# Row softmax on one core: which block of a tile's rows a partition takes

## The chip, the cores and the metric

The kernel runs on one core of a Trainium2 chip. The time is that of the device, in microseconds. A run is told by its median over repeated executions; the profile is of one execution. The core has 128 partitions of on-chip memory, VectorE (DVE in the profile), ScalarE (ACT), GpSimd (POOL) and SyncE (SP), and sixteen DMA engines that move data between the chip's memory and the partitions. TensorE is not used.

## The reference

The input is 32 x 512 rows of 1024 float32 numbers, so 16384 rows and 67.11 MB; the output has the same shape. Each row is divided by the temperature 0.5 and put through a softmax:

```python
scaled = x / temperature
shifted = scaled - np.max(scaled, axis=-1, keepdims=True)
exp_x = np.exp(shifted)
return (exp_x / np.sum(exp_x, axis=-1, keepdims=True)).astype(np.float32)
```

A row needs nothing of another row, so it doesn't matter which partition works on it, if the result goes back to its place.

## The kernel before

The 16384 rows are cut into eleven tiles, one after the other in memory: ten of 1536 rows and a last one of 1024 (`PASSES`, L10). A tile has 128 partitions with 12 rows (the last: 8) in each, 48 KB (32 KB) a partition. Four buffers hold tiles (`BUFS`, L11); a result overwrites its input in the buffer.

`dram(t, i)` (L50) gives the part of the input or the output that belongs to tile i, as partitions x rows x columns. Partition p takes the p-th block of 12 rows, so that the 128 blocks lie in memory in the order of the partitions and the tile is one contiguous stretch of 6144 KB (4096 KB). Both the load (L60) and the store (L108) use it, with one DMA for each tile.

Compute goes in groups of 4 or 6 rows per partition. `maximum` (L63) reduces each row on VectorE (L69) and scales the result into a bias (L72); `exponential` (L74) runs one ScalarE instruction per row (L78), with the row's sum as a by-product; `divide` (L87) takes reciprocals (L90) and multiplies on VectorE, in one instruction for a group (L93) in some tiles and row by row (L96) in the others.

The order is written out by hand (L113 to L127). Four loads are issued at the start. Then each group's maximum and exponential are followed by the division of the group before; in the last two tiles, for their first groups, that division comes ahead. When a tile's last group is divided, `store` issues its store, from GpSimd's queue for the first six tiles and from ScalarE's queue for the last five, and then `load()` issues the load of the next tile on SyncE's queue, which waits until the store that frees the buffer has landed. Ahead of the first store, a one-column copy on GpSimd (L106) holds that queue until the third tile has arrived.

Of the kernel before, what the change touches and what calls it, by code (L numbers as in the profile page):

```python
# [1 line left out]

# [4 lines left out]

PASSES = [[4, 4, 4]] + [[6, 6]] * 9 + [[4, 4]]  # L10
BUFS = 4  # L11

WHOLE = (2, 3, 4, 6, 8)


BY_POOL = 6

ALONE = 9


@with_exitstack
def kernel(
    ctx: ExitStack,
    tc: tile.TileContext,
    x: bass.AP,
    temperature: bass.AP,
    out: bass.AP,
):
    nc = tc.nc
    f32 = mybir.dt.float32  # L30
    scale = 1.0 / float(temperature)
    extreme = mybir.AluOpType.max if scale > 0 else mybir.AluOpType.min

    P = 128
    xf = x.flatten_outer_dims()
    of = out.flatten_outer_dims()
    n, d = xf.shape
    rows = [sum(ks) for ks in PASSES]
    assert sum(rows) * P == n

    data = ctx.enter_context(tc.tile_pool(name="data", bufs=BUFS))
    stats = ctx.enter_context(tc.tile_pool(name="stats", bufs=4))


    groups = []
    for i, ks in enumerate(PASSES):
        for j, k in enumerate(ks):
            groups.append((i, sum(ks[:j]), k))

    def dram(t, i):  # L50
        block = t[P * sum(rows[:i]) : P * sum(rows[: i + 1]), :]
        return block.rearrange("(p k) d -> p k d", p=P, k=rows[i])

    tiles, small = [], []

    def load():
        i = len(tiles)
        if i < len(PASSES):
            xt = data.tile([P, rows[i], d], f32, name="xt")
            nc.sync.dma_start(out=xt, in_=dram(xf, i))  # L60
            tiles.append(xt)

    def maximum(g):  # L63
        i, a, k = groups[g]
        top, bias, sums, recip = (
            stats.tile([P, k], f32, name=name) for name in ("top", "bias", "sums", "recip")
        )
        small.append((bias, sums, recip))
        nc.vector.tensor_reduce(  # L69
            out=top, in_=tiles[i][:, a : a + k, :], axis=mybir.AxisListType.X, op=extreme  # L70
        )
        nc.vector.tensor_scalar_mul(bias, in0=top, scalar1=-scale)  # L72

    def exponential(g):  # L74
        i, a, k = groups[g]
        bias, sums, _ = small[g]
        for b in range(k):
            nc.scalar.activation(  # L78
                tiles[i][:, a + b, :],
                tiles[i][:, a + b, :],  # L80
                mybir.ActivationFunctionType.Exp,
                bias=bias[:, b : b + 1],
                scale=scale,
                accum_out=sums[:, b : b + 1],
            )

    def divide(g):  # L87
        i, a, k = groups[g]
        _, sums, recip = small[g]
        nc.vector.reciprocal(recip, sums)  # L90
        if i in WHOLE:
            xt = tiles[i][:, a : a + k, :]
            nc.vector.tensor_mul(xt, xt, recip.unsqueeze(2).to_broadcast([P, k, d]))  # L93
            return
        for b in range(k):
            nc.vector.tensor_scalar_mul(  # L96
                tiles[i][:, a + b, :], in0=tiles[i][:, a + b, :], scalar1=recip[:, b : b + 1]
            )

    def store(g):  # L100
        i, a, k = groups[g]
        if a + k == rows[i]:
            if i == 0:


                nc.gpsimd.tensor_copy(stats.tile([P, 1], f32, name="seen"), tiles[2][:, 0, 0:1])  # L106
            queue = nc.gpsimd if i < BY_POOL else nc.scalar
            queue.dma_start(out=dram(of, i), in_=tiles[i])  # L108
            load()

    with tc.manual_schedule():  # L113
        for _ in range(BUFS):
            load()
        for g in range(len(groups) + 1):

            alone = g < len(groups) and groups[g][0] >= ALONE and groups[g][1] == 0
            if g > 0 and alone:
                divide(g - 1)  # L120
                store(g - 1)
            if g < len(groups):
                maximum(g)
                exponential(g)
            if g > 0 and not alone:
                divide(g - 1)
                store(g - 1)  # L127


# [1 line left out]
_INS = ['x', 'temperature']  # L131
_OUTS = [((32, 512, 1024), 'float32')]

_NUMBERS = {'temperature': 0.5}


# [26 lines left out]
```

## Time and profile before

| what | value |
|---|---|
| median of 3 runs | 317.14 us (317.06 to 317.22) |
| span of the profiled execution | 315.8 us |
| bytes read and written | 67.11 MB and 67.11 MB |
| mean rate over the span | 425 GB/s |
| load of 6144 KB, issue to landing | 36.4 us (median of 10) |
| store of 6144 KB, issue to landing | 35.9 us (GpSimd's queue), 31.9 us (ScalarE's) |
| last store (4096 KB), issue to landing | 13.5 us |

The span runs from the first to the last instruction of one profiled execution; the runs' median is 1.3 us longer. In the profile a queue is named by a number: q1 carries SyncE's loads, q0 GpSimd's stores, q10 ScalarE's stores. A packet is a piece that one DMA engine moves at a time. The row marked DMA gives, for 40 equal slices of the span, the mean busy share of the sixteen DMA engines in tenths. In the table by stretches, the columns after the interval are its length, the busy time and number of instructions of VectorE, ScalarE and GpSimd, the granted clock, the DMA engines' busy share and the rate in GB/s; a packet is counted where it starts, so that a short stretch's rate and share (1.05, say) are rough by a packet on each engine.

### The profile page before, as it was taken

To read this page: it belongs to the slowest core of one execution; us is meant where nothing else is said; L and a number is where in the kernel's file an instruction comes from. 1 tells how busy PE (TensorE), PEld (TensorE's weight loads), DVE (VectorE), ACT (ScalarE), POOL (GpSimd) and SP (SyncE) were. 2 spreads that over 40 slices of the span, in tenths; PEclk is the share of its full clock that TensorE was granted. 3 is DMA by queue.
4 is the path that set the end of the run, shared out by engine and by line. 5 is a ranking of instruction groups with operands and counts; after the bars stand their busy time and mean duration, and the time that the engine had idled before them with its cause. 6 is when DMAs were issued, how large, how long until landed. Compare 5 with 4: busy or idle time off the path is not lost.

```text
span 315.8 us, 525 instructions
## 1 busy us (share of the span) xinstructions
DVE 256.9 (81%) x147; ACT 148.3 (47%) x257; POOL 3.7 (1%) x11
## 2 busy tenths in 40 slices
DVE  0069999999999899979976994999199999969710
ACT  0029636775461807344471744074416802953700
POOL 0000001000000000000000000000000000000000
DMA  8999999999999999999999999999999999999996
GB/s 305 473 417 423 461 411 399 399 468 430 400 479 417 417 461 411 430 467 405 442 448 399 455 442 405 467 424 417 461 417 430 455 401 463 411 452 411 455 411 270
DMA packets 3171, 134.24 MB, mean 425 GB/s; under 512 B 352, under 2 KB 352, under 8 KB 352
## 3 DMA queue, kind: packets, MB, share of 16 engines
q1 hardware_dynamic: 1584, 67.11, 49.7%
q0 software_dynamic: 864, 37.75, 27.6%
q10 hardware_dynamic: 720, 29.36, 21.5%
q14 instruction: 3, 0.02, 0.0%
HBM read 67.11 MB, written 67.11 MB: 425 GB/s over the span
## 4 chain that ended last, share of the span: by engine, by line
DMA 47%; DVE 28%; ACT 11%; issue 9%; DVEq 0%; SPq 0%; POOLq 0%
DMA xt<-in_x_dram 25%; DMA out_dram<-xt 22%; DVE top L69 16%; ACT xt L78 11%; DVE xt L96 8%; DVE xt L93 2%; DVE bias L72 0%; DVE recip L90 0%; DVEq L158 0%; SPq L60 0%; POOLq L108 0%
## 5 line engine op out<-in xcount | busy, mean ns | idle before, releaser
L78 ACT ACTIVATE xt<-xt,bias 128x1024 f32<-128x1024 f32 x128 | 145.2, 1135 | 131.7 <-DVE recip L90 70.6
L69 DVE TENSOR_REDUCE top<-xt 128x6 f32<-128x6144 f32 (+1 forms) x23 | 139.9, 6083 | 37.8 <-DMA xt<-in_x_dram 37.8
L93 DVE TENSOR_TENSOR xt<-xt,recip 128x6144 f32<-128x6144 f32 x10 | 65.6, 6558 | 0.4
L96 DVE TENSOR_SCALAR xt<-xt,recip 128x1024 f32<-128x1024 f32 x68 | 46.2, 749 | 0.5
L78 ACT ACTIVATION_READ_ACCUMULATOR xt<-xt,bias 128x1 f32 x128 | 23.9, 187 | 0.0
L78 ACT ACT_TABLE_LOAD x1 | 1.3, 1283 | 18.3 <-DMA xt<-in_x_dram 18.3
L90 DVE RECIPROCAL recip<-sums 128x6 f32<-128x6 f32 (+1 forms) x23 | 4.2, 182 | 5.0 <-ACT xt L78 5.0
L108 POOL DMA_DIRECT2D out_dram<-xt x6 | 3.3, 554 | 129.6 <-ACT xt L78 82.7
L72 DVE TENSOR_SCALAR bias<-top 128x6 f32<-128x6 f32 (+1 forms) x23 | 3.9, 171 | 0.8
L106 POOL COPY seen<-xt 128x1 f32<-128x1 f32 x1 | 0.2, 185 | 46.9 <-DMA xt<-in_x_dram 46.9
L144 POOL MEMSET const-uint8-127<- 128x1 uint8 x1 | 0.1, 103 | 0.0
L144 POOL MEMSET const-bfloat16-1.0<- 128x1 bf16 x1 | 0.1, 102 | 0.0
L144 POOL MEMSET const-float32-0.0<- 128x1 f32 x1 | 0.1, 99 | 0.2 <-issue 0.2
L144 POOL MEMSET const-float32-1.0<- 128x1 f32 x1 | 0.1, 98 | 0.0
## 6 DMA issues: line engine op xcount, KB each, us to landing
xt<-in_x_dram SPq DMA_DIRECT2D x10, 6144.0 KB, 36.4
out_dram<-xt POOLq DMA_DIRECT2D x6, 6144.0 KB, 35.9
out_dram<-xt ACTq DMA_DIRECT2D x4, 6144.0 KB, 31.9
xt<-in_x_dram SPq DMA_DIRECT2D x1, 4096.0 KB, 34.9
out_dram<-xt ACTq DMA_DIRECT2D x1, 4096.0 KB, 13.5
```

Source lines behind the costliest of these rows:

```text
L69: nc.vector.tensor_reduce(out=top, in_=tiles[i][:, a : a + k, :], axis=mybir.AxisListType.X, op=extreme)
L72: nc.vector.tensor_scalar_mul(bias, in0=top, scalar1=-scale)
L78: nc.scalar.activation(tiles[i][:, a + b, :], tiles[i][:, a + b, :], mybir.ActivationFunctionType.Exp, bias=bias[:, b : b + 1], scale=scal ...
L90: nc.vector.reciprocal(recip, sums)
L93: nc.vector.tensor_mul(xt, xt, recip.unsqueeze(2).to_broadcast([P, k, d]))
L96: nc.vector.tensor_scalar_mul(tiles[i][:, a + b, :], in0=tiles[i][:, a + b, :], scalar1=recip[:, b : b + 1])
L106: nc.gpsimd.tensor_copy(stats.tile([P, 1], f32, name="seen"), tiles[2][:, 0, 0:1])
L108: queue.dma_start(out=dram(of, i), in_=tiles[i])
L144: nc = _bacc.Bacc("TRN2", target_bir_lowering=False, num_devices=1)
```

## The change

Within a tile, partition 4q + r (r from 0 to 3, q from 0 to 31) takes block 32r + q, where it took block 4q + r. So four neighbouring partitions take blocks that are 32 blocks apart, and the partitions 0, 4, 8 and so on take blocks 0, 1, 2 and so on. A block is still 12 (8) whole rows, contiguous in memory and in the partition. The load and the store use the same view, so each row goes back to where it came from. For the DMAs the rows and columns of a partition are merged into one dimension; on the memory's side the 128 partitions become two dimensions, 32 by 4.

```diff
     def dram(t, i):
         block = t[P * sum(rows[:i]) : P * sum(rows[: i + 1]), :]
-        return block.rearrange("(p k) d -> p k d", p=P, k=rows[i])
+        return block.rearrange("(r q k) d -> q r (k d)", r=4, q=P // 4, k=rows[i])
...
             xt = data.tile([P, rows[i], d], f32, name="xt")
-            nc.sync.dma_start(out=xt, in_=dram(xf, i))
+            nc.sync.dma_start(out=xt.rearrange("p k d -> p (k d)"), in_=dram(xf, i))
             tiles.append(xt)
...
             queue = nc.gpsimd if i < BY_POOL else nc.scalar
-            queue.dma_start(out=dram(of, i), in_=tiles[i])
+            queue.dma_start(out=dram(of, i), in_=tiles[i].rearrange("p k d -> p (k d)"))
             load()
```

## The prediction

> **What bounds the kernel now.** I read the page's busy times and DMA rows first, then the table of stretches of time, then the waits of SyncE's DMA queue, then the rows of the DMA issues.
>
> The page, its busy times and its DMA part:
>
> ```profile
> span 315.8 us, 525 instructions
> DVE 256.9 (81%) x147; ACT 148.3 (47%) x257; POOL 3.7 (1%) x11
> ...
> DMA  8999999999999999999999999999999999999996
> ...
> q1 hardware_dynamic: 1584, 67.11, 49.7%
> q0 software_dynamic: 864, 37.75, 27.6%
> q10 hardware_dynamic: 720, 29.36, 21.5%
> ...
> HBM read 67.11 MB, written 67.11 MB: 425 GB/s over the span
> ```
>
> No compute engine is full, VectorE at 81% least far from it; the DMA row is at 9 in every slice but the first and the last, and the three queues' shares add to 98.8%. The 11 loads of q1 have 1584 packets, 144 each: 128, one per partition, and 16 more, one for each of the 16 DMA engines. So a packet is a partition's whole row in the tile, 48 KB, and all sixteen engines take part in each transfer.
>
> The table by stretches (busy time of VectorE, ScalarE and GpSimd, the clock, the DMA engines' busy share, GB/s):
>
> ```profile
> 0.00:10.00 10.00, 0.00 (x0) 0.00 (x0) 0.21 (x4) 1.00 0.90 354
> 10.00:20.00 10.00, 1.75 (x1) 1.28 (x1) 0.00 (x0) 1.00 1.00 433
> 20.00:40.00 20.00, 19.65 (x17) 13.80 (x24) 0.00 (x0) 1.00 1.00 433
> 40.00:60.00 20.00, 19.86 (x17) 12.70 (x23) 0.85 (x2) 1.00 1.00 413
> 60.00:290.00 230.00, 206.14 (x104) 112.22 (x195) 2.66 (x5) 1.00 1.00 434
> 290.00:310.00 20.00, 9.46 (x12) 8.33 (x16) 0.00 (x0) 1.00 0.99 428
> 310.00:315.80 5.80, 0.00 (x0) 0.00 (x0) 0.00 (x0) 1.00 0.47 203
> ```
>
> This carries the forecast. Loads alone (10 to 40 us), loads with stores (60 to 290) and stores alone (290 to 310) all move 428 to 434 GB/s with the engines busy: one ceiling, whatever the mix. At 434 the 134.24 MB take 309.3 us. The missing 6.5 us of the span can be placed by (1 - rate/434) of each stretch: 1.84 us in the first ten (1.0 of them idle, the share being 0.90; 0.84 busy but slow), 0.97 from 40 to 60 us with the engines fully busy, where the first store (issued at 47.9 us) meets the loads, 0.28 from 290 to 310, 3.09 at the end, 0.07 elsewhere: 6.25, near enough. Only the two slow places, 0.84 and 0.97, can depend on which memory address an engine is at.
>
> The waits of SyncE's DMA queue and the issues:
>
> ```profile
> SPq L60 <- DMA out_dram<-xt: 241.2, 7, 74.3
> ```
>
> ```profile
> L60 SPq DMA_DIRECT2D xt<-in_x_dram x11: 327/328/682, 0.7 to 246.7; - x11
> ...
> L108 POOL DMA_DIRECT2D out_dram<-xt x6: 531/533/665, 47.9 to 179.9; - x6
> L108 ACTq DMA_DIRECT2D out_dram<-xt x5: 338/338/972, 211.2 to 301.3; - x5
> ```
>
> Each load past the fourth waits for the store that frees its buffer, and then takes 36.4 us to land: the buffers are a closed circle of transfers that share one ceiling. Compute has slack inside it.
>
> The profiled execution spans 315.8 us; the median of the runs is 317.14, so 1.3 us more than the span, which I leave as they are. My sum is of differences, added to the median.
>
> **The change, part by part.** Removed and added instructions: none. 11 loads and 11 stores stay, with the same bytes (6144 KB, the last 4096), on the same queues and behind the same waits; no wait is added, so nothing is newly queued behind one. Every row still passes through one partition, so the 23 reductions, 128 exponentials and 78 multiplications keep their shapes and times: 0 us, not by cover but because they are the same.
>
> Memory side. In a 12-row tile a partition's rows are 48 KB in memory. Now neighbouring partitions hold neighbouring blocks; afterwards a step of one partition inside a group of four is 32 blocks, 1.5 MB (1 MB in the 8-row last tile), and a step from one group to the next is 48 KB. Each packet stays one contiguous 48 KB, so I expect the same 144 packets and no smaller pieces. The rate in mid-kernel is the same for reads, for writes and for both, and in the last stretch with 32 KB blocks too (428): the row nearest to a new order of blocks is this one, in which the order has mattered to nothing once transfers are under way. I take 0 us. Bounds: if every one of the 309.3 us ran as the slow first stretch did while busy (354/0.90 = 393 GB/s), the bytes would take 341.6 us, +32.3; if both slow places became clean, -1.8.
>
> One rule speaks against the change. The Trainium skill, DMA: Bandwidth & Descriptors, section "Latency and other measured facts", reports copies whose partitions lie 512 KiB apart at 207 GB/s a direction and 2 MiB apart at 164, with 214 as the full rate. Laid on our 1.5 MB, that would be an estimate of +10.5 us (309.3 x (214/207 - 1)) to +94 us (309.3 x (214/164 - 1)), so 328 to 411 us. I don't take it: its steps are powers of two across all partitions, whereas here only groups of four are that far apart. No row of this profile shows such a step.
>
> Issue side. The memory address now needs two counters (32 by 4 blocks) where one of 128 did. An issue is 0.33 us on SyncE's queue, 0.34 on ScalarE's and 0.53 on GpSimd. SyncE's time is the same for the 4096 KB load as for the others (327 least, 328 median), so I take nothing for a second counter; the bound below is nothing as well, since no step of an issue is dropped, and the bound above is one more of the same length. Exposed are only the first load (0.33) and the last store (0.34, on ScalarE): +0.67 us. The other issues lie behind transfers of 13.5 to 71.1 us in flight; without that cover it would be 10 x 0.33 + 4 x 0.34 + 6 x 0.53 = 7.8 us more. ScalarE's four earlier stores would hold its exponentials for 0.34 us each, beside 131.7 us of its idle time.
>
> Split over the DMA engines. The 16 closing packets of each transfer say that all engines share it now; the trace doesn't say how partitions are dealt to them, nor that it stays so. Bounds: as now, 0; half of them effective at a time, 134.24 MB at 217 GB/s, +309 us. I take 0, by the packet row, and keep the other end as a rival. On this the same page ("Why a DMA increments its semaphore by 16 and not by 1") says that the count is the largest up to 16 that divides the outermost counts of both sides; for 128 and 32 that is 16, hence no change by that rule; it doesn't settle which partitions share an engine.
>
> Sum for the likeliest case: 0 + 0 + 0 + 0, with +0.1 us rounded in for the longer walk at the two exposed issues (inside its 0 to 0.67): 317.2 us. Its own range is 316.5 to 317.8.
>
> **The rivals.**
>
> Faster: the two slow places clear. For it: from 0 to 10 and from 40 to 60 us the engines are busy and under the ceiling just where sixteen engines begin a new kind of transfer together; those are moments at which start addresses could collide, and the change places them anew. Against it: a first packet has a latency of its own, and 40 to 60 us can be the first store's setting up, neither of which has to do with blocks. Worth at most 0.84 + 0.97 = 1.8 us: 315.3. Below 0.63 us it can't be told from no change, since 0.2% of 317 is about what a measurement of this kernel can tell.
>
> Slower, at every start (the other side): the new steps make the sixteen engines collide whenever a transfer begins, not just at the two places. Price: 0.84 and 0.97, mean 0.905 us, on the 20 other transfers, +18.1: 335.2; if half of them pay, 326.2. It decides from 0.63 us on, less than one start in all, because no idle DMA time in the middle can take it up. For it: a ceiling with no reserve; any slower packet lengthens the end. Against it: 20 of the 22 starts now show nothing of the kind, and the transfers of the middle overlap, so that engines don't begin together.
>
> Slower, by the split: with a memory side counted as 32 by 4, the partitions are dealt to the engines in another way, and engines get in each other's way. If only loads alone (to 47.9 us) and stores alone (from 246.7 + 34.9 = 281.6 to 315.8) go at half rate, that is 48 + 34 = 82 us more, 399; if all does, 626. For it: nothing in the profile guards against it, and the present rate is at the ceiling of all sixteen. Against it: 128 divides into four and 32 evenly. By the skill's SBUF — State Buffer, "Door 1: The DMA port swizzle", four neighbouring partitions share a port, and the groups of four stay whole here, which speaks for an unchanged split.
>
> That the change does nothing at all to the addresses is excluded: every partition but the first and the last takes another block.
>
> **How the numbers follow.** Unchanged 0.37, at 317.2 (316.5 to 317.8). Faster 0.20, down to 315.3. Slower at starts 0.26, 317.8 to 349.4, middle 326. Slower by the split 0.17, 399 to 626. The range is 315.2 to 335: it holds the first two and most of the third, and leaves out the split with the last 0.03 of the third. Faster 0.20, same 0.37, slower 0.26 + 0.17 = 0.43.
>
> **What would show it.** Right: 144 packets in each transfer, mid-kernel 434 GB/s at a share of 1.00, issues of 0.33, 0.53 and 0.34 us, and the same two slow places. Faster: more than 354 GB/s in the first ten us or more than 413 from 40 to 60. Slower at starts: a share of 1.00 with a mid-kernel rate of 410 to 430. The split: half the rate in the load-only stretch from 10 to 40 us, with the engines' share at 1.00, or engines idle there. A rate below 434 in mid-kernel with unchanged packet counts would make me wrong about the order of blocks; an idle share there would make me wrong about the split or the issue.

## The result and the profile after

The changed kernel takes 317.87 us in the median of 16 runs (317.11 to 320.22), the kernel before beside it 317.20 (316.99 to 317.68). The ratio is 1.0027, with a 95% interval of 1.0015 to 1.0040: slower by a quarter of a per cent, inside the forecast range of 315.2 to 335, but just outside both the 0.2% that was called no change and the likeliest case's own range (316.5 to 317.8). On two other chips, where the kernel before itself had runs up to 321.4, the ratio was 0.9999 (0.9977 to 1.0021) and 0.9987 (0.9956 to 1.0019).

The page of the kernel after, span and queues:

```profile
span 316.1 us, 525 instructions
...
q1 hardware_dynamic: 1584, 67.11, 49.6%
q0 software_dynamic: 864, 37.75, 27.6%
q10 hardware_dynamic: 720, 29.36, 21.5%
...
HBM read 67.11 MB, written 67.11 MB: 425 GB/s over the span
```

The packets are the same, 144 a transfer. Its table by stretches (columns as before):

```profile
0.00:10.00 10.00, 0.00 (x0) 0.00 (x0) 0.20 (x4) 1.00 0.81 329
10.00:20.00 10.00, 1.81 (x1) 1.28 (x1) 0.00 (x0) 1.00 1.06 457
20.00:40.00 20.00, 19.65 (x17) 13.80 (x24) 0.00 (x0) 1.00 1.00 433
40.00:60.00 20.00, 19.86 (x17) 12.76 (x23) 0.86 (x2) 1.00 0.98 393
60.00:290.00 230.00, 205.88 (x104) 111.94 (x195) 2.71 (x5) 1.00 1.00 434
290.00:310.00 20.00, 9.68 (x12) 8.55 (x16) 0.00 (x0) 1.00 0.99 427
```

Mid-kernel nothing moved: 434 GB/s at a share of 1.00, to the digit. The first ten us have more idle time (share 0.81, was 0.90), and the next ten count more (329 and 457 average to 393, as 354 and 433 did); the place where the first store meets the loads is 393, was 413. A packet counts where it starts, so these short stretches are rough.

The rows of the DMA issues (least, median and longest time in ns):

```profile
L60 SPq DMA_DIRECT2D xt<-in_x_dram x11: 534/535/717, 0.7 to 246.8; - x11
...
L108 POOL DMA_DIRECT2D out_dram<-xt x6: 542/543/676, 47.8 to 179.9; - x6
L108 ACTq DMA_DIRECT2D out_dram<-xt x5: 546/546/1591, 211.2 to 301.6; - x5
```

This is the clear difference of the two profiles: an issue takes 207 ns more on SyncE's queue (328 to 535), 208 on ScalarE's (338 to 546) and only 10 on GpSimd (533 to 543). In the trace's packet records, the first load's first packet starts at 1.76 us before and 2.12 after. Yet that load ends no later, if its end is the moment at which the last of the sixteen engines is done. Steps of the chain of waits, before:

```profile
0.74 17.48 DMA xt<-in_x_dram
...
190.44 38.06 DMA xt<-in_x_dram
...
228.52 6.56 DVE top L69
```

and after:

```profile
0.73 17.43 DMA xt<-in_x_dram
...
190.50 38.20 DMA xt<-in_x_dram
...
228.73 6.56 DVE top L69
...
300.21 1.32 DVE xt L96 x2
```

The first load takes 17.43 us against 17.48. But each engine closes its share of a load with a small packet of its own, and the mean of the sixteen closing packets of the first load comes at 17.52 us after and 17.31 before: most engines are later, though the last one isn't. Further down, the ninth tile's load is in at 228.7 us (228.5 before), and from there to the last store's issue at 301.6 the chain consists of compute alone. The chain follows the last instruction, not the DMA engines. By the packet records these are without a packet for less than 0.01 us from 290 to 308 us, in either profile: they are still at the store before the last when the last store is issued.

### The profile page after: what moved, and what is told of

Same layout as the page of the kernel before. It is cut to its first block, busy times and chain, and to the rows that moved or that the text cites. A ratio compares the mean times of both kernels' runs of the same rounds, so it can differ in the third digit from the quotient of the medians.

```text
span 316.1 us, 525 instructions
## 1 busy us (share of the span) xinstructions
DVE 256.9 (81%) x147; ACT 148.3 (47%) x257; POOL 3.8 (1%) x11
## 4 chain that ended last, share of the span: by engine, by line
DMA 47%; DVE 28%; ACT 11%; issue 9%; DVEq 0%; SPq 0%; POOLq 0%
DMA xt<-in_x_dram 24%; DMA out_dram<-xt 22%; DVE top L69 16%; ACT xt L78 11%; DVE xt L96 8%; DVE xt L93 2%; DVE bias L72 1%; DVE recip L90 0%; DVEq L158 0%; SPq L60 0%; POOLq L108 0%
```

## The experiments

Three theories were held against each other. Theory 1, the issue: two counters make each issue longer, and the first load's and the last store's are on the path that sets the end. Theory 2, the order: other places in memory make transfers slower. Theory 3 came with the first results: single executions are long because one DMA engine falls behind the others.

For theory 3 the runs are read in two bands. Nearly every kernel here has executions near 317.5 us and others near 320. The limit of 318.9 between them is a choice: few runs lie near it, but there is no gap (318.82, 318.86, 318.97 and 319.02 all occur). Below, "short" is the median of the runs under 318.9, as a difference to the short median of the kernel before on the same chip, and "long" counts the others.

| kernel | new blocks in | short, us | long runs |
|---|---|---|---|
| before (four chips) | none | 0 | 0/16, 10/35, 8/23, 11/29 |
| after (three chips) | all | +0.54, +0.30, +0.53 | 3/16, 0/12, 2/12 |
| two counters, old order but for neighbours | none | +0.76 | 5/12 |
| old at both ends | tiles 2 to 10 | -0.30, -0.45 | 0/11, 1/12 |
| new at both ends only | tiles 1 and 11 | +0.59 | 7/12 |
| loads new | loads | +0.33 | 4/12 |
| stores new | stores | +0.01 | 0/12 |
| 64 by 2 | all, larger step | +0.12 | 1/10 |

The short differences are small beside their spread. When the runs are resampled, 95% of the differences lie between 0.35 and 0.76 us for the changed kernel on the first chip, between -0.20 and 0.71 and between 0.12 and 0.92 on the others, between -0.05 and 0.58 for loads new, -0.26 and 0.29 for stores new and -0.12 and 1.19 for new at both ends, which has only five short runs. The packet records separate the kernels better. For each profile, this is when the first load's first packet starts, when the sixteen engines close the first load (mean, and the last one), and the mean of the sixteen closings of the last store:

| profile of | counters at the first load | first packet, us | first load closed, mean | last engine | last store closed, mean |
|---|---|---|---|---|---|
| before | one | 1.76 | 17.31 | 17.89 | 313.39 |
| stores new | one | 1.75 | 17.32 | 18.15 | 313.45 |
| old at both ends, twice | one | 1.75, 1.76 | 17.29, 17.32 | 17.96, 18.27 | 313.54, 313.44 |
| after, three times | two | 2.12, 2.12, 2.13 | 17.52, 17.57, 17.61 | 17.83, 17.84, 18.03 | 313.95, 314.00, 314.08 |
| loads new | two | 2.12 | 17.60 | 17.78 | 313.86 |
| form alone (a long run) | two | 2.14 | 17.63 | 18.18 | 315.61 |
| new at both ends (a long run) | two | 2.46 | 17.56 | 18.02 | 316.98 |
| 64 by 2 (with late engines) | two | 2.13 | 17.59 | 17.95 | 314.36 |

With two counters at the first load its first packet is 0.36 us later (0.70 in one profile), the sixteen engines close that load 0.2 to 0.3 us later in the mean, and among the first eight profiles of the table the last store is closed 0.3 to 0.7 us later in the mean. The two groups don't overlap, and the counters of the other transfers and the change's order of blocks make no difference that shows. (The version below with steps of 512 KB and one counter starts at 1.76 us as well but closes its first load at 17.52, with slower packets.) In between, from 20 to 308 us, those eight profiles have no more than 0.13 us in which an engine has no packet (mean of the sixteen), so there is no idle time that could take up a late start. The time at which the last engine closes the first load doesn't sort the kernels.

**The changed kernel again, twice.**

> The changed kernel once more, to see whether its spread belongs to it: its 16 runs lay between 317.11 and 320.22 us, those of before between 316.99 and 317.68. Both theories expect a ratio of 1.0027 (1.0015 to 1.0040). If the spread comes from the new places in memory, some runs are again above 319 us; if it was chance, all lie within 0.7 us of each other, as before.

Median 317.87 (317.31 to 318.74), none above 319. The spread was not the changed kernel's own: the kernel before beside it reached 321.1.

> The changed kernel a third time, beside before on the same chip. Theory 1 (the cost of the issue, seen in the short band): its short runs lie 0.3 to 0.5 us above those of before (317.74 to 317.20 and 317.87 to 317.57 so far). Theory 3: at most 2 of 12 runs long (3 of 28 so far), and before more often. With both, the medians lie within 0.3% of each other either way.

318.25 (317.40 to 320.16), 2 of 12 long, before 11 of 29. The short band is 0.53 us above that of before, a little over what theory 1 expected; the short medians lie 0.3 to 0.5 us higher on each of three chips, on one of them within the spread, while the whole comparison was even on the last two, since there the kernel before had more long runs.

**The form alone.**

```diff
-        return block.rearrange("(r q k) d -> q r (k d)", r=4, q=P // 4, k=rows[i])
+        kd = rows[i] * d
+        b4 = block.rearrange("(q r k) d -> q r (k d)", r=4, q=P // 4, k=rows[i])
+        return bass.AP(tensor=b4.tensor, offset=b4.offset + 3 * kd,
+                       ap=[[4 * kd, P // 4], [-kd, 4], [1, kd]])
```

> The memory side is walked by two counters, 32 by 4, as in the changed kernel, but the blocks hardly move: partition 4q + r takes block 4q + 3 - r, so only the order inside a group of four neighbours is turned round. Theory 1, the issue: with two counters a DMA issue on SyncE's and ScalarE's queues takes 0.21 us longer (0.327 to 0.534 and 0.338 to 0.546 in the two profiles), which lengthens the time by 0.2 (last store) to 0.4 us (first load too): 317.4 to 317.6. Theory 2, the order in memory: nothing, 317.2, because nearly the same addresses are read and written at the same time. Either way the issues should show 0.53 and 0.55 us.

318.81 (317.81 to 320.49), ratio 1.0030 (1.0003 to 1.0057); issues of 535, 542 and 547 ns. The form without the new order costs as much as the change or more: short +0.76, against +0.30 for the changed kernel on the same chip. Theory 2 fails as the cause of the loss. That the new order gives something back is possible, but seven and twelve short runs don't show it.

The profiled run of this kernel was a long one, 320.12 us, and shows what a long run is. Its chain of waits and its table by stretches:

```profile
191.29 40.33 DMA xt<-in_x_dram
...
231.64 6.56 DVE top L71
```

```profile
60.00:290.00 230.00, 203.36 (x102) 111.68 (x196) 2.71 (x5) 1.00 1.01 435
290.00:310.00 20.00, 12.56 (x14) 9.16 (x16) 0.00 (x0) 1.00 0.89 386
```

The rate up to 290 us is full, 435 GB/s. But the ninth tile's load takes 40.33 us and is in at 231.6 instead of 228.5, the compute chain of some 73 us starts that much later, the last store is issued at 304.5, and the DMA engines run dry ahead of it: a share of 0.89, and by the packet records 1.7 us without a packet from 300 to 308 us (mean of the sixteen). In the trace's records of the sixteen closing packets of a load, the last comes 4.0 to 5.3 us after the eighth for the ninth to eleventh loads of this run. In the other long profile (new at both ends, 321.21 us) it is 5.1 to 6.1 us; in the eight profiles of the 317 to 318 us class (before, after, its two repeats, both of old at both ends, loads new, stores new) it is 0.4 to 1.3. So one engine closes each of these loads well behind the others; the second latest comes 1.0 to 1.5 us after the eighth. After 60 us these two traces have single packets that take 0.1 to 0.9 us more than the usual 1.8, most of them of loads. That these set the one engine back is likely but not shown, since the records name no engine. Nor does the limit of 318.9 divide cleanly: the profiled run of 64 by 2, at 318.75 us a short one, has three closing packets 2.3 to 4.1 us behind the eighth.

**Old blocks at both ends, and the reverse.**

```diff
         block = t[P * sum(rows[:i]) : P * sum(rows[: i + 1]), :]
+        if i in (0, len(PASSES) - 1):   # the reverse: not in
+            return block.rearrange("(p k) d -> p (k d)", p=P, k=rows[i])
         return block.rearrange("(r q k) d -> q r (k d)", r=4, q=P // 4, k=rows[i])
```

> The first and the last tile take their blocks as before, with one counter; the nine tiles between them are as in the changed kernel. The two issues on the path that sets the end are then short again. Theory 1, the issue: 317.2, as before, with a narrow spread. Theory 2, the order in memory: 317.6 to 317.9, with runs above 319 us, as in the changed kernel, since 18 of 22 transfers have the new order.

317.27 (316.97 to 317.85), ratio 0.9975 (0.9952 to 0.9998): faster than the kernel before.

> The reverse: only the first and the last tile take their blocks in the new way, so only their two loads and two stores have the longer issue. Theory 1, the issue: the whole loss, 317.4 to 317.9. Theory 2, the order in memory: 317.2, or up to 317.3 for 4 of 22 transfers; should the new order matter only at the first load, a change of at most the 0.84 us that the first ten us lost.

320.00 (317.46 to 321.29), ratio 1.0046 (1.0014 to 1.0077). With four transfers changed out of 22 the whole loss is there, short +0.59; with eighteen changed and these four not, there is none. That points at the two ends, as theory 1 says, though on five short runs. That more than half the runs were long was expected by nobody.

> Old blocks with one counter in the first and the last tile, new blocks in the nine between, once more. So far the runs fall into two bands: a short one around 317.5 us and a long one around 320 (above 318.9). Long were 18 of 58 runs of the kernel before on the last two chips (0 of 16 on the first), 16 of 36 of the kernels whose middle stores keep the old order, but only 3 of 51 of those whose middle stores write the new blocks (after, ends_old, stores_new). Theory 3 (a late DMA engine, and the new order of the stores makes it rarer): at most 1 of 12 runs long, short band around 317.3, median below that of before by 0.2 to 0.7 us if before has its long runs again. Chance: 3 or 4 of 12 long.

317.17 (316.87 to 319.81), ratio 0.9955 (0.9925 to 0.9985), 1 of 12 long. This version beats the kernel before on both chips (by 0.45% here), and the medians of the changed kernel beside it are 317.87 and 318.25; why its short runs lie below those of before isn't shown. Its issues in the profile, with the short one at an end of each queue as the least value:

```profile
L62 SPq DMA_DIRECT2D xt<-in_x_dram x11: 336/535/1032, 0.7 to 246.2; - x11
...
L110 ACTq DMA_DIRECT2D out_dram<-xt x5: 353/547/1718, 210.8 to 301.0; - x5
```

The short ones, 336 and 353 ns, also have the rows and columns of a partition merged, as the change does. So it is the second counter and not the merging that adds the 0.2 us.

**Loads alone, stores alone.** In these two the other direction keeps the old blocks, so rows come out permuted within a tile.

```diff
+        if t is of:     # loads new; stores new: t is xf
+            return block.rearrange("(p k) d -> p (k d)", p=P, k=rows[i])
```

> Only the loads take the new blocks, the stores write as before; the rows of a tile therefore come out in another order within the tile, and nothing else differs. Theory 1, the issue (two counters cost 0.21 us an issue, exposed at the first load and the last store): only the first load is late, by 0.2 to 0.36 us (its first packet came at 1.76 us before and 2.12 after): 317.4 to 317.6, less whatever the new order gives back at the start. Theory 2, the order in memory: part of 0.5 to 0.9 us. Theory 3, late engines: in the long executions of either kernel (about 320 us) one DMA engine closes its share of the loads 4 to 8 us after the others, and the last tiles' compute then starts late; how often that happens is chance or hangs on the order, and the spread of these runs shows which. First landing as after, 17.8 us.

318.01 (317.37 to 319.87), ratio 0.9997 (0.9967 to 1.0028). Short +0.33, the first landing at 17.78 us as expected, 4 of 12 long like before (8 of 23).

> Only the stores write the new blocks, the loads read as before; again rows come out in another order within the tile. Theory 1: only the last store's issue is exposed, +0.21 to 0.31 us: 317.4 to 317.5, the first landing as before at 17.9 us. Theory 2: part of 0.5 to 0.9 us, from the place where the first store meets the loads (before: 413 GB/s from 40 to 60 us). Theory 3 as for the loads.

317.50 (317.10 to 318.08), ratio 0.9966 (0.9940 to 0.9991). The last store's longer issue, 547 ns in this profile too, does not show: short +0.01, where 0.21 to 0.31 was expected. So of the two ends the first load is the one that costs, as the table of closings says too. None of 12 was long.

Why the last store's issue is free can be read from the packet records. In the eight profiles that are not of long runs its first packet starts 1.6 to 2.4 us after the issue begins, and the packets of the store before it end only at 304.3 to 305.4 us, some 3.5 us after that issue: the engines are not waiting for it. Where some had run dry, the first packet came 0.85 us after the issue with one counter (the 512 KB version below) and 1.20 to 1.28 us with two (form alone, 64 by 2, new at both ends). That is the first load's 0.36 us again, only now nobody has to pay it unless a late engine has let the others run dry.

**A larger step with one counter.**

```diff
-        block = t[P * sum(rows[:i]) : P * sum(rows[: i + 1]), :]
-        return block.rearrange("(p k) d -> p k d", p=P, k=rows[i])
+        block = t.rearrange("(p m) d -> p m d", p=P)
+        return block[:, sum(rows[:i]) : sum(rows[: i + 1]), :]
```

> One counter, but a quite different order in memory: each partition owns 128 consecutive rows of the whole input, so that in every load and store neighbouring partitions are 512 KB apart, where it was 48 KB. If the order doesn't matter once transfers are under way (theory 1), 316.9 to 317.5, with 434 GB/s from 60 to 290 us. If an order with large steps costs, as theory 2 needs, 320 us or more; the figure that the Trainium skill has for such a step (DMA: Bandwidth & Descriptors, 'Latency and other measured facts', 207 of 214 GB/s at 512 KiB) would make 328.

323.8 (322.38 to 326.72, 4 runs), ratio 1.0141 (1.0076 to 1.0206). Its table by stretches, in a run of 326.72 us:

```profile
60.00:290.00 230.00, 199.34 (x99) 111.67 (x196) 2.67 (x5) 1.00 1.00 427
290.00:310.00 20.00, 16.60 (x17) 9.17 (x16) 0.00 (x0) 1.00 0.84 361
```

Here the order does cost in mid-kernel: 427 GB/s (in the longest of the four runs), and then more by late engines (up to 8.7 us) and a dry tail. The rule that was weighed in the prediction, from the Trainium skill, DMA: Bandwidth & Descriptors, "Latency and other measured facts", has the right sign for 512 KiB. Its 207 of 214 is 3.3% less; the rate here fell by 1.6%.

**Other counts: 16 by 8 and 64 by 2.**

```diff
-        return block.rearrange("(r q k) d -> q r (k d)", r=4, q=P // 4, k=rows[i])
+        return block.rearrange("(r q k) d -> q r (k d)", r=8, q=P // 8, k=rows[i])
```

> The change with 16 by 8 in place of 32 by 4: partition 8q + r takes block 16 r + q. The issue has two counters as in the changed kernel, so theory 1 expects the changed kernel's time, 317.4 to 317.9. The rival on the split: groups of eight cannot be dealt to the sixteen engines as groups of four can; if engines then get in each other's way, loads alone (10 to 40 us) run at about half of 433 GB/s and the time is 399 to 626 us.

471.4 us (468.9 to 475.8), ratio 1.480 (1.471 to 1.490). The table:

```profile
10.00:45.00 35.00, 10.53 (x7) 7.44 (x12) 0.00 (x0) 1.00 1.01 209
60.00:290.00 230.00, 145.37 (x71) 81.78 (x143) 3.44 (x7) 1.00 1.00 299
```

Each transfer still has 144 packets, sixteen of them closing ones, and all engines are busy, at half the rate when only loads run, and at two thirds when loads and stores mix: the rival on the split, at a neighbouring count. The control turns each group of eight round, with `r=8`, `7 * kd` and the step `-kd` in the edit of the form alone:

> 16 by 8 counters with nearly the old order in memory: partition 8q + r takes block 8q + 7 - r. The 16 by 8 version with new blocks took 471 us and moved 209 GB/s from 10 to 45 us. If the split over the DMA engines is the cause, this takes 450 to 490 us as well, with about 209 GB/s in that stretch; if the order in memory was the cause, 317 to 319 us and 433 GB/s.

478.9 us in two runs, ratio 1.501 (1.490 to 1.511), and the same stretch:

```profile
10.00:45.00 35.00, 10.44 (x7) 7.35 (x12) 0.00 (x0) 1.00 1.00 208
```

So it is the count, not the place in memory. The 64 by 2 version has `r=2, q=P // 2`:

> 64 by 2 counters: partition 2q + r takes block 64 r + q, so neighbours are 3 MB apart in a 12-row tile, twice the changed kernel's step. If an outer count of 64 or 32 keeps the split over the engines and only 16 breaks it, 317.2 to 320 us with 434 GB/s from 60 to 290 us and issues of 0.53 us on SyncE's queue; if any outer count but 32 and 128 breaks it, above 400 us. By the skill's figures for large steps (164 of 214 GB/s at 2 MiB) it would be over 400 us as well, but with a lower rate in the middle rather than in the load-only stretch alone.

317.87 (317.23 to 319.40), ratio 0.9983 (0.9951 to 1.0014); mid-kernel 435 GB/s, issues of 535 ns on SyncE's queue. Neighbours 3 MB apart cost nothing that these runs show. Counts of 32 and 64 leave the split harmless, 16 doesn't.

By the Trainium skill's SBUF — State Buffer, "Door 1: The DMA port swizzle", eight consecutive partitions lie on two ports, and partitions 32 apart share one. If at 16 by 8 each engine were given eight consecutive partitions, the engines would meet in pairs on a port. The half rate fits that, but it is a guess: no trace here shows which engine had which partition.

## Why the prediction was right or wrong

**What bounds the kernel: right, but with little reserve at the end.** 434 GB/s was a ceiling and stayed one, and in the eight profiles that are not of long runs the engines have no gap up to 308 us. The sentence that "compute has slack inside it" holds for these, but in the last tiles the slack is small: from the ninth tile's load at 228.5 us to the last store's issue at 301.4 the chain is compute alone, and the store before the last ends only some 3.5 us later. By the long profiles, a ninth load that is in 3.1 or 4.4 us later uses that up and comes out as time (form alone and new at both ends, with 1.7 and 2.3 us without a packet from 300 to 308 us); one that is 1.8 us later begins to (64 by 2, 0.4 us).

**The order of blocks at 0 us: right in mid-kernel for this change.** Mid-kernel rates are equal. As a general reading of that table it was too bold: 512 KB steps with one counter cost 1.4%. At the two slow places no effect of the order is shown either. The stretch from 40 to 60 us reads 393 for 413 also with the form alone, which has nearly the old order, and 401 and 413 with the old blocks at both ends and the new ones between; so it goes with the late start of the first load and not with the order.

**The issue at +0.1 us: the term that was mis-sized.** I took nothing for a second counter because SyncE's time was the same for a smaller load. That row spoke of the size of the rows, not of the number of counters. Measured are +0.207 us an issue on SyncE's queue and +0.208 on ScalarE's, two thirds of the upper bound of one more of the same length, but the first packet is 0.36 us later, more than the issue alone, so the price of what follows an issue was missing from the bound. At the first load it is paid in full: the engines are busy from there to the last store, and the mean closing of the last store is 0.3 to 0.7 us later. The kernel with the two ends put back, its reverse, loads alone and stores alone agree with that in their short medians. The part on the last store failed: that issue was called exposed, but it lies behind the store before it.

**The rivals.** Faster, by clearing the slow places: not seen. The first load's last engine lands no later in spite of a late start, but the mean of the sixteen does. Slower at every start: refuted by the equal mid-kernel rate. Slower by the split: not here, but real at 16 by 8, at 471 us inside its 399 to 626. The reason given against it, that 128 divides into four and 32 evenly, was no protection: 16 by 8 divides evenly as well.

**The forecast.** "Unchanged" at 0.37 was the likeliest, with 317.2 us and a range up to 317.8. Measured is 317.87, by +0.27% past the 0.2% and just inside the numbers of the rival "slower at starts" (317.8 to 349.4). That is no merit of that rival, whose mechanism isn't there: one start is late, by its issue, and no other shows it. The term that did it was in the sum, with 0.1 us in place of 0.3 to 0.5, inside its bound of 0.67 us; but that bound came out by luck, since it left out what follows an issue and counted the last store, which costs nothing. What wasn't seen at all is the third effect: kernels that write the new blocks in the middle tiles had 6 long runs in 75 (after, old at both ends, stores new; 64 by 2 had 1 in 10, and three more just under the limit), those with two counters somewhere but the old order in the middle stores 16 in 36, and the kernel before 29 in 87 on the same three later chips. These counts speak for it that the new order of the stores makes a late engine rarer, and it held in the runs made to test it (1 and 2 of 12 long, beside 11 of 29); why it would is open. Against it stands the first chip, where it was the other way round (0 of 16 before, 3 of 16 after), which made the changed kernel's mean there worse than its short band. Together with the limit of 318.9, which was chosen after the first runs, this leaves it likely and not shown.

## What to carry to other kernels

A memory view with a second counter has a price at each DMA issue; it matters only where nothing covers it, here at the first load, so keep the plain view there. Whether a start is late is better read from the mean of the engines' closing packets than from the last one. Before an outer count is chosen, measure it: 32 and 64 were harmless, 16 halved the rate with every engine busy. At a DMA ceiling, look also at the spread among the engines that close a transfer, since whoever waits for the transfer waits for the last one.

## What the runs showed of the hardware

- A DMA issue with two counters on the memory side takes 0.535 us on SyncE's queue and 0.546 on ScalarE's instead of 0.328 and 0.338. On GpSimd it takes 0.543 instead of 0.533 for 32 by 4, but 0.608 for 64 by 2 and 0.524 for 16 by 8. The first packet of a transfer that meets idle engines comes 0.36 us later (2.12 us for 1.76).
- An outer count of 16 against 128 partitions moves 209 GB/s in loads alone where 32, 64 and 128 move 433.
- One DMA engine can close its loads 4 to 6 us behind most of the others within a kernel of 318 us (form alone, new at both ends), and what waits for its share pays.
